# Softmax over 32,768 columns on one core: two pieces of 8192 a tile, one half scaled by VectorE and the other by ScalarE, stores at the end of the tile

## Chip, cores, metric

One core of a Trainium2 chip. The metric is device time in microseconds (us). The engines are named as the profile names them: DVE is VectorE, ACT is ScalarE, POOL is GpSimd, SP is SyncE; SPq and ACTq are their queues that issue DMA transfers.

## The reference

```python
logits: float32 [16, 256, 32768], temperature = 1.0
scaled = logits / temperature
scaled = scaled - scaled.max(axis=-1, keepdims=True)
e = np.exp(scaled)
out = e / e.sum(axis=-1, keepdims=True)
```

Every element is read once and written once: 536.87 MB in, 536.87 MB out.

## The kernel before

The 4,096 rows are cut in halves of 16,384 columns, one half to a partition, so 64 tiles of 128 x 16384 (8.39 MB). Three buffers take turns. For each piece of a tile DVE finds the negated maximum and ACT takes the exp in place with its sum. Then the two halves of a row are combined by a few one-column operations, and the pieces are scaled in place, partly by DVE and partly by ACT.

```python
_BUFS = 3
_LOAD = (8192, 8192)                    # loads of a tile, columns
_PIECES = (4096, 4096, 4096, 4096)      # pieces for max and exp
_ON_DVE = (4096, 1024, 4096, 1024)      # of each piece, scaled by DVE; ACT has the rest
_HALF = 8192                            # a store
...
    for k in range(K):                  # per piece
        nc.vector.tensor_reduce(out=nm[:, k:k+1], in_=xc, axis=X, op=A.max, negate=True)
        nc.scalar.activation(out=xc, in_=xc, func=Exp, bias=nm[:, k:k+1],
                             scale=inv_t, accum_out=ssum[:, k:k+1])
    ...                                 # small steps -> f[:, k], one factor a piece
    for k in range(K):
        a, b, c = at[k], at[k] + on_dve[k], at[k] + sizes[k]
        if b > a: nc.vector.tensor_scalar_mul(out=xs[:, a:b], in0=xs[:, a:b], scalar1=f[:, k:k+1])
        if c > b: nc.scalar.activation(out=xs[:, b:c], in_=xs[:, b:c], func=Copy, scale=f[:, k:k+1])
        if t == G - 1: store(t, a, c)
        elif t and c % _HALF == 0: store(t, c - _HALF, c)     # on ACT's queue
...
    for t in range(G):
        normalise(t)
        if t and t + _BUFS - 1 < G:
            load(t + _BUFS - 1)         # on SP's queue, into the buffer of tile t - 1
```

The first and last tile have cuts of their own, which the change leaves alone.

## Time and profile before

| | before |
|---|---|
| median, four runs | 2,493.23 us (2,493.11 to 2,493.26) |
| span in the profile | 2,491.5 us |
| DVE / ACT busy | 1580.1 us (63%) / 1352.5 us (54%) |
| DMA | 431 GB/s, both queues together 100.0% of the 16 engines' time |
| one tile in mid-run | 38.7 us |

The page, the chain of waits and the groups by form stand in the prediction. One more view: the timeline of one tile's scaling (start, length, engine, operation).

```profile
480.57 5.94 DVE L148 TENSOR_SCALAR x<-x,f 128x4096 f32<-128x4096 f32 x4
480.62 2.86 ACT L152 ACTIVATE x<-x,f 128x3072 f32<-128x3072 f32 x1 [1.15 <-DVE f L144]
483.66 0.34 ACTq L81 DMA_DIRECT2D out_dram<-x  x1
484.05 2.86 ACT L152 ACTIVATE x<-x,f 128x3072 f32<-128x3072 f32 x1 [0.56 <-DVE x L148]
...
486.93 0.34 ACTq L81 DMA_DIRECT2D out_dram<-x  x1
```

The four DVE scalings take 5.94 us together. The first store is issued when both engines have finished the first half, 3.27 us before the second store.

### The profile page before, as it was taken

The numbers are of one execution on the slowest core, as the hardware profiler recorded it, in microseconds if no ns is written. First come the engines' busy times: TensorE is split into PE (matmuls) and PEld (weight loads), VectorE is DVE, ScalarE is ACT, GpSimd is POOL, SyncE is SP. The second block draws the span as 40 slices with busy tenths as digits, with TensorE's granted clock in tenths as the row PEclk, the third lists the DMA queues.
The fourth block names the chain that finished last, engine by engine and source line by source line (L and its number), as shares of the span: only waits on it lengthen the run. The fifth ranks groups of instructions, "written<-read, shape, count | busy, mean of one in ns | idle before, by whom it ended". The sixth has DMA issues, their size and how long they took to land.

```text
span 2491.5 us, 2807 instructions
## 1 busy us (share of the span) xinstructions
DVE 1580.1 (63%) x1217; ACT 1352.5 (54%) x711; POOL 0.2 (0%) x4
## 2 busy tenths in 40 slices
DVE  7765666655766657566675666756667566665654
ACT  6565555655556555555555554555545555465544
POOL 0000000000000000000000000000000000000000
DMA  9999999999999999999999999999999999999998
GB/s 412 436 430 436 431 435 431 433 433 430 437 430 437 430 436 430 437 429 436 431 436 431 434 432 432 434 431 436 430 437 429 437 430 436 430 437 430 436 431 370
DMA packets 38038, 1073.94 MB, mean 431 GB/s; under 512 B 4224, under 2 KB 4224, under 8 KB 4224
## 3 DMA queue, kind: packets, MB, share of 16 engines
q1 hardware_dynamic: 20160, 553.66, 51.6%
q10 hardware_dynamic: 17856, 520.10, 48.4%
q14 instruction: 22, 0.18, 0.0%
HBM read 536.87 MB, written 536.87 MB: 431 GB/s over the span
## 4 chain that ended last, share of the span: by engine, by line
DMA 68%; another core or an unknown queue 15%; DVE 11%; ACT 4%; issue 1%; SPq 0%; ACTq 0%
DMA out_dram<-x 41%; DMA x<-in_logits_dram 28%; DVE nm L108 8%; ACT x L115 3%; DVE x L148 3%; SPq L72 0%; DVE f L144 0%; ACT x L152 0%; ACT ee L129 0%; DVE rS L143 0%; DVE Sh L91 0%; DVE Sh L88 0%; DVE ttj L132 0%; ACTq L197 0%
## 5 line engine op out<-in xcount | busy, mean ns | idle before, releaser
L108 DVE TENSOR_REDUCE nm<-x 128x1 f32<-128x4096 f32 (+1 forms) x257 | 1119.1, 4395 | 639.0 <-DMA x<-in_logits_dram 639.0
L115 ACT ACTIVATE x<-x,nm 128x4096 f32<-128x4096 f32 (+1 forms) x257 | 949.3, 3694 | 976.4 <-DVE nm L108 976.0
L152 ACT ACTIVATE x<-x,f 128x3072 f32<-128x3072 f32 (+1 forms) x132 | 366.4, 2781 | 129.9 <-DVE f L144 73.5
L148 DVE TENSOR_SCALAR x<-x,f 128x1024 f32<-128x1024 f32 (+3 forms) x256 | 379.9, 1548 | 2.3
L132 DVE CUSTOM_DVE_ANT_0 ttj<-ee,ssum 128x4 f32<-128x4 f32 x64 | 10.4, 162 | 228.2 <-ACT ee L129 228.2
L115 ACT ACTIVATION_READ_ACCUMULATOR x<-x,nm 128x1 f32 x257 | 47.9, 186 | 0.0
L129 ACT ACTIVATE ee<-nm,nMh 128x4 f32<-128x4 f32 x64 | 18.0, 282 | 0.0
L144 DVE TENSOR_SCALAR f<-ee,rS 128x4 f32<-128x4 f32 x64 | 14.7, 229 | 2.2
L143 DVE RECIPROCAL rS<-Sh 128x1 f32<-128x1 f32 x64 | 10.5, 164 | 2.2
L91 DVE TENSOR_TENSOR Sh<-Sh 128x1 f32<-128x1 f32 x64 | 10.2, 159 | 2.2
L91 DVE TENSOR_TENSOR nMh<-nMh 128x1 f32<-128x1 f32 x64 | 10.2, 159 | 2.2
L127 DVE TENSOR_REDUCE nMh<-nm 128x1 f32<-128x4 f32 x64 | 10.0, 157 | 2.2
L88 DVE STREAM_SHUFFLE Sh<-Sh 128x1 f32<-128x1 f32 x64 | 9.7, 151 | 0.0
L88 DVE STREAM_SHUFFLE nMh<-nMh 128x1 f32<-128x1 f32 x64 | 9.7, 151 | 0.0
L115 ACT ACT_TABLE_LOAD x1 | 1.3, 1283 | 8.1 <-DMA x<-in_logits_dram 8.1
L132 DVE DVE_READ_ACCUMULATOR2_ANT Sh<- 128x1 f32 x64 | 5.2, 82 | 0.0
L88 DVE LOAD_MASK_SELECT nMh<-nMh x64 | 0.9, 14 | 2.8
L88 DVE LOAD_MASK_SELECT Sh<-Sh x64 | 0.9, 14 | 2.8
L183 POOL MEMSET const-bfloat16-1.0<- 128x1 bf16 x1 | 0.1, 101 | 0.0
L183 POOL MEMSET const-uint8-127<- 128x1 uint8 x1 | 0.1, 101 | 0.0
L183 POOL MEMSET const-float32-0.0<- 128x1 f32 x1 | 0.1, 98 | 0.2 <-issue 0.2
L183 POOL MEMSET const-float32-1.0<- 128x1 f32 x1 | 0.1, 98 | 0.0
## 6 DMA issues: line engine op xcount, KB each, us to landing
x<-in_logits_dram SPq DMA_DIRECT2D x124, 4096.0 KB, 31.3
out_dram<-x ACTq DMA_DIRECT2D x124, 4096.0 KB, 49.3
x<-in_logits_dram SPq DMA_DIRECT2D x7, 2048.0 KB, 20.6
out_dram<-x SPq DMA_DIRECT2D x2, 4096.0 KB, 33.5
out_dram<-x SPq DMA_DIRECT2D x3, 2048.0 KB, 17.3
x<-in_logits_dram SPq DMA_DIRECT2D x2, 1024.0 KB, 36.1
out_dram<-x SPq DMA_DIRECT2D x2, 1024.0 KB, 22.8
```

The costliest lines, as they stand in the source:

```text
L88: nc.vector.stream_shuffle(out=v[:, j + 1 : j + 2], in_=v[:, j : j + 1], mask=mask)
L91: nc.vector.tensor_tensor(out=v[:, j + 1 : j + 2], in0=v[:, j : j + 1], in1=v[:, j + 1 : j + 2], op=op,)
L108: nc.vector.tensor_reduce(out=nm[:, k : k + 1], in_=xc, axis=X, op=A.max, negate=True)
L115: nc.scalar.activation(out=xc, in_=xc, func=Exp, bias=nm[:, k : k + 1], scale=inv_t, accum_out=ssum[:, k : k + 1],)
L127: nc.vector.tensor_reduce(out=nMh[:, 0:1], in_=nm, axis=X, op=A.min)
L129: nc.scalar.activation(out=ee, in_=nm, func=Exp, bias=nMh[:, n_rounds : n_rounds + 1], scale=-1.0)
L132: nc.vector.tensor_tensor_reduce(out=ttj, in0=ee, in1=ssum, scale=1.0, scalar=0.0, op0=A.mult, op1=A.add, accum_out=Sh[:, 0:1],)
L143: nc.vector.reciprocal(out=rS, in_=Sh[:, n_rounds : n_rounds + 1])
L144: nc.vector.tensor_scalar_mul(out=f, in0=ee, scalar1=rS)
L148: nc.vector.tensor_scalar_mul(out=xs[:, a:b], in0=xs[:, a:b], scalar1=f[:, k : k + 1])
L152: nc.scalar.activation(out=xs[:, b:c], in_=xs[:, b:c], func=Copy, scale=f[:, k : k + 1])
L183: nc = _bacc.Bacc("TRN2", target_bir_lowering=False, num_devices=1)
```

## The change

The intent, in the words that came with it: two column pieces of 8192 a tile, one half scaled by VectorE, the other by ScalarE; loads and stores in 32 KB halves (per partition) on two hardware queues. Fewer and longer instructions, and no half that waits for both engines.

```diff
-_PIECES = (4096, 4096, 4096, 4096)
-_ON_DVE = (4096, 1024, 4096, 1024)
+_PIECES = (8192, 8192)
+_ON_DVE = (8192, 0)
 _HALF = 8192
+_SECOND_PIECES = (4096, 4096, 4096, 4096)
+_SECOND_ON_DVE = (4096, 4096, 2048, 0)
@@ the cuts of a tile
+        if t == 1:
+            return _SECOND_PIECES, _SECOND_ON_DVE, _LOAD
         return _PIECES, _ON_DVE, _LOAD
@@ the end of normalise
-            elif t and c % _HALF == 0:
-                store(t, c - _HALF, c)
+        for h in range(0, W if 0 < t < G - 1 else 0, _HALF):
+            store(t, h, h + _HALF)
```

(The width of the small tiles, `K`, also takes in the second tile's cut.)

More of the change, by code (lines that the diff above doesn't have):

```diff
@@ L48 @@
     n_rounds = _SPLIT.bit_length() - 1
-    K = max(len(_FIRST_PIECES), len(_PIECES), len(_LAST_PIECES))
+    K = max(
+        len(p) for p in (_FIRST_PIECES, _SECOND_PIECES, _PIECES, _LAST_PIECES)
+    )
     pool = ctx.enter_context(tc.tile_pool(name="fixed", bufs=1))
```

## The prediction

> **What bounds the kernel now.** I first read the page's busy shares, its slices and its DMA queues.
>
> ```profile
> DVE 1580.1 (63%) x1217; ACT 1352.5 (54%) x711; POOL 0.2 (0%) x4
> ...
> DMA  9999999999999999999999999999999999999998
> GB/s 412 436 430 436 431 435 431 433 433 430 437 430 437 430 436 430 437 429 436 431 436 431 434 432 432 434 431 436 430 437 429 437 430 436 430 437 430 436 431 370
> ...
> q1 hardware_dynamic: 20160, 553.66, 51.6%
> q10 hardware_dynamic: 17856, 520.10, 48.4%
> ...
> HBM read 536.87 MB, written 536.87 MB: 431 GB/s over the span
> ```
>
> No compute engine is busy for two thirds of the span. The 16 DMA engines are at 90% or more in every slice but the last, and the packets of the two queues add up to 51.6 + 48.4 = 100.0% of the engines' time. Only the first and last slices (412 and 370 GB/s) are clearly below the rest. So DMA is the bound, and I ask whether a queue is ever empty. For that I read the DMA queue's own waits and, for two rounds of the three buffers, the chain that ended last.
>
> ```profile
> SPq L72 <- DMA out_dram<-x: 2339.5, 122, 47.8
> ...
> 367.60 48.28 DMA out_dram<-x
> ...
> 416.34 18.89 another core or an unknown queue
> ...
> 435.35 31.34 DMA x<-in_logits_dram
> ...
> 466.71 8.76 DVE nm L108 x2
> ...
> 475.49 3.80 ACT x L115 x2
> ...
> 480.57 3.03 DVE x L148 x2
> ...
> 483.66 48.37 DMA out_dram<-x
> ```
>
> The first row says that SyncE spends nearly the whole run waiting for a store to free a buffer. The pieces (start, length) give the loop: a first-half store issued at 367.60 lands at 415.9; the queue then issues a first-half load (0.33 us), and 18.89 us later the second-half load at 435.35, because the second-half store has landed; that load takes 31.34 us; two maxima, an exp, the small steps and scaling follow, and the next store goes at 483.66. From 367.60 to 483.66 three tiles have passed: 38.69 us a tile. A tile moves 16.777 MB (1,073.74 MB over 64), so the rate in this stretch is 16.777 / 38.69 = 433.6 GB/s.
>
> **Slack.** Loads are issued at 416.01, 435.35, 454.69 and 474.04 (the timeline of SyncE's queue): 19.35 us apart, which is what a 4.19 MB half takes when two queues share 433.6 GB/s (4.19 / 0.2168 = 19.35). A load that lands after 31.3 us has therefore queued for 12.0. A first-half store takes 48.3 us, so it has queued for 29. A second-half store is issued about 3.3 us later (448.24 against 444.97 in the timeline) and lands 19.3 us later than its first half, so it takes about 64.4 and has queued for 45. Both queues have a backlog at every moment; the stores' is the longer, by far.
>
> [...]Two hardware queues were in use already, with the same 4 MB halves.[...]
>
> **The change, part by part.** The durations come from the groups by form:
>
> ```profile
> L108 DVE TENSOR_REDUCE nm<-x 128x1 f32<-128x4096 f32 x255 | 1114.7, 4412 | 639.0 <-DMA x<-in_logits_dram 639.0
> L115 ACT ACTIVATE x<-x,nm 128x4096 f32<-128x4096 f32 x255 | 945.3, 3707 | 976.4 <-DVE nm L108 976.0 <-ACT x L152 0.5
> L152 ACT ACTIVATE x<-x,f 128x3072 f32<-128x3072 f32 x124 | 354.0, 2856 | 127.6 <-DVE f L144 71.2 <-DVE x L148 34.1 <-DMA x<-in_logits_dram 22.4
> L148 DVE TENSOR_SCALAR x<-x,f 128x4096 f32<-128x4096 f32 x124 | 291.4, 2350 | 2.2
> L148 DVE TENSOR_SCALAR x<-x,f 128x1024 f32<-128x1024 f32 x124 | 92.7, 747 | 0.0
> ```
>
> Each operation has a constant and a slope. Max: 4412 at 4096 and 2275 at 2048 (last tile) give 1.043 ns an element, so 8.69 us at 8192. Exp: 3707 and 1986 give 0.840, so 7.15 us. DVE scaling: 2350 and 747 give 0.522, so 4.49 us. ACT scaling: 2856 at 3072 and 1564 at 1536 give 0.841, so 7.16 us.
>
> (1) Engine work for each of the 61 tiles from the third to the one before the last. DVE before: 4 x 4.41 + 2 x 2.35 + 2 x 0.75 = 23.85; after: 2 x 8.69 + 4.49 = 21.87; 1.98 less, 121 us in the run, so DVE should fall to about 1,459 us. ACT before: 4 x (3.71 + 0.19 for reading the accumulator) + 2 x 2.86 = 21.29; after: 2 x (7.15 + 0.19) + 7.16 = 21.84; 0.55 more, 34 us, so about 1,386. Five instructions go on each engine in each of these tiles, and one more on DVE in the second tile: DVE 1217 to 911, ACT 711 to 406. None of this is on the path that sets the end.
>
> (2) From the second half's landing to the stores. Before: 483.66 - 466.71 = 17.0 us to the first store, 20.2 to the second. After: max 8.69, exp 7.15, the same 1.4 of small steps (exp end 479.2 to scaling 480.6), then ACT's 7.16: 24.4 us. The first half needs only DVE's 4.49, but both store issues now stand behind ACT's scaling in ACT's program order. So the first store goes 7.5 us later, the second about 4.6 (24.7 against 20.2). This is the only real cost, and it comes out of 29 and 45 us of queueing: about 21 and 40 are left. The landing times, and with them loads and period, do not move. Gain and loss in steady state: 0.
>
> (3) The start: tile 0 and its stores are untouched. Tile 1's stores move from 63.7 and 67.0 to about 66.4, behind tile 0's stores, of which the first lands at 85.0. No gap.
>
> (4) The end: the last tile is untouched. Tile 61's stores wait in ACT's queue for a late load (22.4 us in the row of ACT scaling), and in the changed program the same semaphore wait stands there. In this stretch ACT's copy moves ahead of that wait, which balances the longer exp: tile 62's stores go about 1 us earlier by the same durations. The end is then set by the last load's landing at 2,446.98 us and by the drain. About 0.
>
> (5) A small gain that I assume without proof. Three-tile steps in the chain are of two kinds: 367.60 to 483.66 is 116.06, but 250.45 to 367.60 is 117.15. Eight of the steps are long, 233 or 350 us (two or three steps) apart. The page has 22 instruction transfers on queue 14, and DVE's 1,217 instructions would need one every 262 us if each brought 128[...]. If they cause the extra 0.9 us, 911 instructions have some two or three fewer: 2 us.
>
> Sum: 2,493.3 + 0 + 0 + 0 - 2 = 2,491 us.
>
> **Rivals.** *The later stores starve the DMA engines.* For it: 7.5 us later in each tile would be up to 61 x 7.5 = 458 us if the path were serial, 2,950 us; the chain does run through max, exp and scaling. Against it: the chain's store and load pieces contain 29 and 12 us of queueing, so those steps are not a bound although the chain lists them. *The coarser pieces relieve the engines and give time back.* 121 us off DVE would be 2,372 us[...].[...] *A new bound in an engine*: in series a tile takes DVE 17.4 (maxima) + 7.15 + 1.4 + 4.5 = 30.5 us before the next tile's maximum can start, against the 38.7 of DMA: 8 us remain, so no. *A start or end that drains worse*: the last slice has few transfers left, and a wait that shifts there by some us is paid in full; 5 us either way.
>
> **Range and chances.** [...]the three runs of before differ by 0.06 us, so only the two ends and the long steps can move the time. I take 2,491 with 2,486 to 2,497. A change of 2% is 50 us; [...]a loss needs a starved queue (1%). Within 2%: 98.7%.
>
> **What would show it.** Right: DMA rate and slices as before, 38.7 us a tile; loads still 31.3 us from issue to landing; first-half stores near 41 us instead of 48.3 and second-half ones near 60; DVE near 1,459 and ACT near 1,386 us busy; the wait of SyncE for stores still over 2,300 us. The long steps should come some 350 us apart if instruction transfers cause them. Wrong: slices with DMA under 9 or 420 GB/s in mid-run, a load landing within 20 us of its issue (a queue run dry), or a period above 39 us.

What the page of the kernel before shows is that packets take 100.0% of the DMA engines' time and that no slice exceeds 437 GB/s. The 128 instructions a transfer of step (5) were assumed there; the trace of the changed kernel shows 126 to 130 (below).

## The result, and the profile after

| | before | after |
|---|---|---|
| median, four runs each | 2,493.23 us | 2,491.32 us (2,491.30 to 2,491.41) |
| ratio | | 0.9993, 95% interval 0.9975 to 1.001 |
| span in the profile | 2,491.5 us | 2,489.5 us |
| instructions DVE / ACT | 1217 / 711 | 911 / 406 |

A ratio is the mean time of one kernel's fast runs over the mean of the other's fast runs of the same rounds, so it is not quite the ratio of the medians. The kernel is the same within noise; the 1.9 us between the two is far above the scatter of these four runs (0.15 us), and below what the interval resolves.

The page of the changed kernel, busy shares, slices and queues:

```profile
DVE 1483.5 (60%) x911; ACT 1391.5 (56%) x406; POOL 0.2 (0%) x4
...
DMA  9999999999999999999999999999999999999998
GB/s 412 437 430 434 434 431 436 431 436 431 434 432 431 436 430 435 432 434 432 431 436 431 436 430 436 432 431 436 431 435 430 435 432 432 435 432 435 431 433 384
...
q14 instruction: 16, 0.13, 0.0%
...
x<-in_logits_dram SPq DMA_DIRECT2D x124, 4096.0 KB, 31.4
out_dram<-x ACTq DMA_DIRECT2D x124, 4096.0 KB, 44.6
```

DMA looks as before: 90% or more in every slice but the last. The line of q14 counts transfers of the kind that the profile names instruction: 16, where the kernel before had 22. The last two lines give the median time from issue to landing: 31.4 us for loads as before (31.3), and 44.6 for stores in place of 49.3. The two kernels move the same data.

The chain that ended last, two rounds of the three buffers (start, length, what), to be laid beside the piece in the prediction:

```profile
371.39 44.59 DMA out_dram<-x
...
416.36 18.93 another core or an unknown queue
...
435.35 31.38 DMA x<-in_logits_dram
...
466.75 8.70 DVE nm L114
...
475.47 7.21 ACT x L121 x2
...
483.96 4.50 DVE x L154
...
488.48 43.67 DMA out_dram<-x
```

The second-half load is issued at 435.35 in both kernels and lands within 0.04 us of the same moment, 466.75 against 466.71. Between that landing and the first store lie 21.7 us in place of 17.0, and the store then takes 43.7 us in place of 48.4: what the engines took longer, the store queued less. From 371.39 to 488.48 is 117.1 us for three tiles, a long step; the next ends at 604.53, 116.05 later, so 38.7 us a tile as before.

The timeline of the scaling of that tile:

```profile
483.96 4.49 DVE L154 TENSOR_SCALAR x<-x,f 128x8192 f32<-128x8192 f32 x1
484.02 7.12 ACT L158 ACTIVATE x<-x,f 128x8192 f32<-128x8192 f32 x1 [1.15 <-DVE f L150]
...
488.48 3.03 ACTq L87 DMA_DIRECT2D out_dram<-x  x2
```

The first store is issued at 488.48, the moment DVE's scaling ends, while ACT is still busy with its own until 491.14. The store instruction stands behind that ACTIVATE in ACT's program, and yet it is issued 2.66 us before the ACTIVATE ends. The second store follows at 491.17, when ACT's scaling is done (the row merges the two).

The end of the run, in stretches of 2 us (the last two columns are the DMA share and GB/s); first before, then after:

```profile
2484.00:2486.00 2.00, 0.00 (x0) 0.00 (x0) 0.00 (x0) 1.00 0.18 78
2486.00:2488.00 2.00, 0.00 (x0) 0.00 (x0) 0.00 (x0) 1.00 0.17 70
2488.00:2490.00 2.00, 0.00 (x0) 0.00 (x0) 0.00 (x0) 1.00 0.08 33
```

```profile
2482.00:2484.00 2.00, 0.00 (x0) 0.00 (x0) 0.00 (x0) 1.00 0.31 131
2484.00:2486.00 2.00, 0.00 (x0) 0.00 (x0) 0.00 (x0) 1.00 0.18 78
2486.00:2488.00 2.00, 0.00 (x0) 0.00 (x0) 0.00 (x0) 1.00 0.08 33
```

All 16 DMA engines together move 433 GB/s, so one of them moves 27 on average. In the three stretches shown of each run the DMA share is 0.18, 0.17 and 0.08 before, and 0.31, 0.18 and 0.08 after: 16 times the share is 3 to 5 engines' work, then little more than one's. In the changed kernel this tail lies 2 us earlier. The last load lands 2.0 us earlier too (2,445.02 against 2,446.98), and from there both kernels need 44.5 us.

**Where the 1.9 us come from.** The 19 three-tile steps of the chain (from the store issued at 134.26 us before, at 139.14 after) hold eight long ones (about 117.05 us against 116.13) before and six after. They sum to 2,213.8 and 2,212.6 us, 1.1 us of the difference; another 0.9 lies between the last second-half landing in these steps (2,331.08 before, 2,330.06 after) and that of the last load. The packed trace of the changed kernel has each of the 16 transfers as one packet of 8,192 bytes. Seven of them start after 53, 180, 306, 432, 559, 689 and 815 recorded DVE instructions, 126 to 130 apart, so about 128 for each; seven others lie 124 to 131 ACT instructions apart. That they bring the instructions of DVE and of ACT is read from this spacing. The long steps of the changed kernel are 349 or 350 us apart (once 465); 128 instructions at 14 a tile of 38.7 us are 354 us. Before they were 233 or 350 us apart, for a computed 262 at 19 a tile. So the spacing of the long steps fits DVE's instruction count, which the experiments had to test.

### The profile page after: what moved, and what is told of

Same layout as the page of the kernel before. It is cut to its first block, busy times and chain, and to the rows that moved or that the text cites. A ratio compares the mean times of both kernels' runs of the same rounds, so it can differ in the third digit from the quotient of the medians.

```text
span 2489.5 us, 2075 instructions
## 1 busy us (share of the span) xinstructions
DVE 1483.5 (60%) x911; ACT 1391.5 (56%) x406; POOL 0.2 (0%) x4
## 3 DMA queue, kind: packets, MB, share of 16 engines
q10 hardware_dynamic: 17856, 520.10, 48.4%
## 4 chain that ended last, share of the span: by engine, by line
DMA 63%; another core or an unknown queue 15%; DVE 14%; ACT 7%; issue 0%; SPq 0%; ACTq 0%
DMA out_dram<-x 35%; DMA x<-in_logits_dram 27%; DVE nm L114 9%; ACT x L121 6%; DVE x L154 4%; SPq L78 0%; DVE f L150 0%; ACT x L158 0%; ACT ee L135 0%; DVE rS L149 0%; DVE Sh L97 0%; DVE Sh L94 0%; DVE ttj L138 0%; ACTq L203 0%
## 5 line engine op out<-in xcount | busy, mean ns | idle before, releaser
L121 ACT ACTIVATE x<-x,nm 128x8192 f32<-128x8192 f32 (+1 forms) x135 | 913.5, 6767 | 992.0 <-DVE nm L114 976.7
L114 DVE TENSOR_REDUCE nm<-x 128x1 f32<-128x8192 f32 (+1 forms) x135 | 1112.0, 8240 | 531.6 <-DMA x<-in_logits_dram 531.6
L158 ACT ACTIVATE x<-x,f 128x8192 f32<-128x8192 f32 (+2 forms) x71 | 452.5, 6382 | 73.4 <-DVE f L150 73.4
L154 DVE TENSOR_SCALAR x<-x,f 128x8192 f32<-128x8192 f32 (+3 forms) x72 | 291.1, 4052 | 2.3
L138 DVE CUSTOM_DVE_ANT_0 ttj<-ee,ssum 128x2 f32<-128x2 f32 (+1 forms) x64 | 10.3, 161 | 430.3 <-ACT ee L135 430.3
L121 ACT ACTIVATION_READ_ACCUMULATOR x<-x,nm 128x1 f32 x135 | 25.2, 187 | 0.0
L135 ACT ACTIVATE ee<-nm,nMh 128x2 f32<-128x2 f32 (+1 forms) x64 | 17.9, 280 | 0.0
L150 DVE TENSOR_SCALAR f<-ee,rS 128x2 f32<-128x2 f32 (+1 forms) x64 | 14.6, 229 | 2.2
L97 DVE TENSOR_TENSOR Sh<-Sh 128x1 f32<-128x1 f32 x64 | 10.2, 160 | 2.2
L97 DVE TENSOR_TENSOR nMh<-nMh 128x1 f32<-128x1 f32 x64 | 10.2, 159 | 2.2
L133 DVE TENSOR_REDUCE nMh<-nm 128x1 f32<-128x2 f32 (+1 forms) x64 | 9.9, 155 | 2.2
## 6 DMA issues: line engine op xcount, KB each, us to landing
x<-in_logits_dram SPq DMA_DIRECT2D x124, 4096.0 KB, 31.4
out_dram<-x ACTq DMA_DIRECT2D x124, 4096.0 KB, 44.6
```

Of the source, the lines that this page charges most:

```text
L97: nc.vector.tensor_tensor(out=v[:, j + 1 : j + 2], in0=v[:, j : j + 1], in1=v[:, j + 1 : j + 2], op=op,)
L114: nc.vector.tensor_reduce(out=nm[:, k : k + 1], in_=xc, axis=X, op=A.max, negate=True)
L121: nc.scalar.activation(out=xc, in_=xc, func=Exp, bias=nm[:, k : k + 1], scale=inv_t, accum_out=ssum[:, k : k + 1],)
L133: nc.vector.tensor_reduce(out=nMh[:, 0:1], in_=nm, axis=X, op=A.min)
L135: nc.scalar.activation(out=ee, in_=nm, func=Exp, bias=nMh[:, n_rounds : n_rounds + 1], scale=-1.0)
L138: nc.vector.tensor_tensor_reduce(out=ttj, in0=ee, in1=ssum, scale=1.0, scalar=0.0, op0=A.mult, op1=A.add, accum_out=Sh[:, 0:1],)
```

## The experiments

Two theories were open. **Backlog**: both DMA queues always hold queued work, so nothing on the engines reaches the end (against it: the serial chain, in which each step counts). **Instructions**: the remaining 2 us come from fewer transfers of DVE instructions. All kernels gave correct results. "Before" is the kernel before in the same rounds, on the same chip.

| run | median, us | before, us | ratio | 95% interval |
|---|---|---|---|---|
| e1_widths | 2,492.10 | 2,493.24 | 0.9997 | 0.9982 to 1.0011 |
| e2_split | 2,492.94 | 2,493.24 | 0.9998 | 0.9983 to 1.0013 |
| e3_late_stores | 2,496.27 | 2,493.24 | 1.0010 | 0.9994 to 1.0027 |
| e4_two_buffers | 2,615.23 | 2,493.24 | 1.0490 | 1.0469 to 1.0511 |
| e5_dve_plus6us | 2,492.27 | 2,493.49 | 0.9995 | 0.9979 to 1.0012 |
| e6_dve_plus12us | 2,677.65 | 2,493.49 | 1.0739 | 1.0723 to 1.0755 |
| e7_instr_dve | 2,510.84 | 2,493.49 | 1.0072 | 1.0057 to 1.0087 |
| e8_instr_act | 2,503.42 | 2,493.49 | 1.0037 | 1.0022 to 1.0052 |
| e9_instr_pool | 2,495.00 | 2,494.14 | 1.0004 | 0.9986 to 1.0022 |
| e10_small_on_pool | 2,490.55 | 2,494.14 | 0.9986 | 0.9974 to 0.9999 |
| e11_instr_dve_half | 2,502.65 | 2,494.14 | 1.0034 | 1.0021 to 1.0048 |

One run each of e9 and e11 was slow (2,556.8 and 2,556.2 us); it is in the median and not in the ratio. Without it the medians are 2,494.15 and 2,502.6.

### The two parts alone

The widths alone, on the kernel before:

```diff
-_PIECES = (4096, 4096, 4096, 4096)
-_ON_DVE = (4096, 1024, 4096, 1024)
+_PIECES = (8192, 8192)
+_ON_DVE = (5120, 5120)
```

> Only the pieces of 8192 (scaling still shared inside each half, 5120 on DVE and 3072 on ACT, each half stored as soon as it is scaled). Backlog theory (DMA always has queued work, so nothing on the engines reaches the end): 2,491 to 2,493 us, 38.7 us a tile, loads 31.3 us to landing. Rival, serial chain (the 3.4 us longer exp per tile is paid): 61 x 3.4 = 207 us more, 2,700. Instruction theory (0.85 us for each 128 DVE instructions): 15 DVE instructions a tile against 14 in the changed kernel and 19 in the one before, so 2,491.8.

The 0.85 us is an estimate from the recorded 2 us: 306 DVE instructions fewer are 2.4 transfers of 128.

And the scaling split with the stores at the end, pieces of 4096 as before:

```diff
-_ON_DVE = (4096, 1024, 4096, 1024)
+_ON_DVE = (4096, 4096, 0, 0)
@@ the end of normalise: the stores as in the changed kernel
```

> Only the scaling split (first half on DVE, second on ACT) and both stores at the end; pieces stay 4096. Backlog theory: 2,491 to 2,493.5 us. Serial rival: both stores of a tile some 3 to 5 us later, 61 x 1.5 to 61 x 5 more, 2,580 to 2,800. Instruction theory: 17 DVE instructions a tile, 2,492.6.

Both lie within 0.4 us of the number from the instruction count (2,491.8 and 2,492.6 expected, 2,492.1 and 2,492.9 measured), and 87 us and more below every serial figure. The order of four kernels by DVE instructions (911, 969, 1093, 1217) is their order by time (2,491.3, 2,492.1, 2,492.9, 2,493.2). Such small differences are inside the intervals; the order alone proves little, so the doses below are larger.

### How much delay the engines may have

A useless maximum before the scaling, 5632 or 11264 elements wide, in each of 61 tiles of the changed kernel:

```diff
+        if 2 <= t <= G - 2:
+            nc.vector.tensor_reduce(out=junk, in_=xs[:, 0:5632], axis=X, op=A.max)   # e6: 0:11264
         for k in range(K):
             a, b, c = at[k], at[k] + on_dve[k], at[k] + sizes[k]
```

> The changed kernel with a useless max over 5632 elements (5.97 us by the measured 1.06 ns) on DVE before the scaling of each of 61 tiles. Backlog theory: DVE's own cycle grows from 30.4 to 36.4 us, below the 38.7 of DMA, so 2,491.3 to 2,493. Serial rival: 61 x 6.0 = 364 us more, about 2,855.

> The same with 11264 elements (11.9 us). Backlog theory: DVE's cycle of 30.4 becomes 42.3 us, 3.6 above DMA's 38.7, so DVE is the bound: 61 x 3.6 = 220 us more, 2,680 to 2,740, and DVE waits for loads hardly at all. Serial rival: 61 x 11.9, about 3,220.

Six us a tile, 361 us of added DVE time (1844.3 against 1483.5 us busy), cost nothing that can be measured: 2,492.3 us, against 2,491.3 for the changed kernel on another chip. Twelve cost 186 us over the changed kernel. The chain of e6 shows why:

```profile
992.84 17.20 DVE nm L115 x2
...
1010.06 7.21 ACT x L122 x2
...
1018.51 11.80 DVE junk L153
...
1030.34 4.49 DVE x L157
1034.82 8.59 DVE nm L115
```

No DMA is left in it: two maxima, the exp, the added maximum and the scaling follow each other, 41.98 us from 992.84 to 1034.82, and DVE waited only 12.2 us for loads in the whole run (531.6 in the changed kernel). I had expected a cycle of 42.3 and 220 us; with 41.98 the excess is 3.28 us a tile, 200 us for 61; why the run paid 14 us less is not shown. The measured 2,677.7 lies just under the range that I had given (2,680 to 2,740). The bound changed hands where DVE's cycle of 30.4 us plus the addition passes 38.7, between the two doses. So the slack in DVE has the size that the prediction worked out, about 8 us.

### How much delay the stores may have, and what the third buffer does

```diff
 # e3: the stores of a tile after both exps of the next one
+            if 2 <= t <= G - 2 and k == K - 1:
+                for h in range(0, W, _HALF):
+                    store(t - 1, h, h + _HALF)
...
-        for h in range(0, W if 0 < t < G - 1 else 0, _HALF):
+        for h in range(0, W if t == G - 2 else 0, _HALF):

 # e4
-_BUFS = 3
+_BUFS = 2
```

> The changed kernel, but both stores of a tile are issued only when the next tile's second exp has begun, some 26.7 us later for the first half and 24 us for the second. A first-half store of the changed kernel queued 43.7 - 19.35 = 24.3 us, so the store queue now runs dry for a moment in each tile. If DMA needs only one of its two queues filled: 2,491 to 2,497 us, first-half stores 17 to 25 us to landing. If a dry store queue costs time: 2.4 us a tile, about 2,640. Serial rival: 61 x 26.7 more, about 4,100.

> The changed kernel with two buffers of a tile in place of three. Backlog theory: a buffer's loop of two tiles has 77.4 us and needs at least 19.3 us of load, 24.4 of max, exp and scaling and 19.3 of store at the full rate, 63 in all, so it fits: 2,491 to 2,560 us, with shorter times to landing. Rival: the latencies of the trace (31.4 us for loads, 22 of engines, 43.7 to 60 for stores, 116 in all) are real costs that three buffers hide, so two buffers give 116 / 2 = 58 us a tile, about 3,700.

In e3 a store comes some 25 us later in each tile, and the run is 5 us longer, not 150 or 1,600. Its transfers, from issue to landing (median, in us, last):

```profile
x<-in_logits_dram SPq DMA_DIRECT2D x124, 4096.0 KB, 24.2
out_dram<-x ACTq DMA_DIRECT2D x124, 4096.0 KB, 30.5
```

In the changed kernel they are 31.4 and 44.6. The delay came out of the queueing of the stores and partly of the loads, which I had not expected: the stores stayed above the 17 to 25 us that I had given, and the loads queued less. So the work may wait in either queue.

In e4 my estimate was too kind: 2,615 us, above the 2,560 at which I had put the upper end, though nowhere near the 3,700 of the rival. Its queues and transfers:

```profile
q1 hardware_dynamic: 20160, 553.66, 52.4%
q10 hardware_dynamic: 17856, 520.10, 46.1%
...
x<-in_logits_dram SPq DMA_DIRECT2D x124, 4096.0 KB, 19.8
out_dram<-x ACTq DMA_DIRECT2D x124, 4096.0 KB, 25.4
```

A load lands 19.8 us after its issue, near the 19.35 us that a half takes at half the rate: by this estimate there is no queue of loads left. The packets' time is 52.4 + 46.1 = 98.5% of a span of 2,616.9 us, 2,578 us; in the changed kernel it is 100.0% of 2,489.5. So the same bytes took 88 us more packet time, and the DMA engines stood idle for 39 us (1.5%). My sum of 63 us in a loop of 77 had counted neither: with no backlog, the packets themselves took longer. e6 shows the same (48.5 + 46.8 = 95.3% of 2,675.8, so 2,550 us of packets). Why a packet takes longer then is not shown.

### What instruction transfers cost

```diff
+        if 2 <= t <= G - 2:
+            for i in range(28):                                    # e11: 14
+                nc.vector.memset(junk[:, i : i + 1], 0.0)          # e7, e11
+                nc.scalar.activation(out=junk[:, i : i + 1],       # e8 instead
+                                     in_=nMh[:, 0:1], func=Copy)
+                nc.gpsimd.memset(junk[:, i : i + 1], 0.0)          # e9 instead
```

> The changed kernel with 28 useless one-column memsets on DVE in each of 61 tiles (1,708 instructions, 13.3 transfers of 128 instructions). Instruction theory ([...]0.85 us for each transfer): 11 us more, 2,502, with long three-tile steps far more often. Rival (instruction transfers cost nothing and the 2 us came from elsewhere): 2,491 to 2,492.

> The same 28 useless instructions a tile, on ACT. [...]only what goes beyond DVE's is paid: 2,491 to 2,497. If any instruction transfer holds up the whole stream: 2,502. If none does: 2,491 to 2,492.

> The changed kernel with 28 useless one-column memsets a tile on GpSimd (1,708 instructions, 13 transfers more). [...]If every instruction transfer holds up the stream alike: as with DVE's, 2,503 to 2,511. ACT's 28 gave 2,499.6 to 2,504.6, so something between is possible.

> Half the dose of useless DVE instructions, 14 a tile (854 more, 6.7 transfers). Instruction theory at 0.93 us each: 6.2 us more, 2,497.5. If the 28 cost 19.5 us by something else that sets in late (a wait that the memsets bring about): less than half, 2,492 to 2,495, or, in proportion, 2,501.

The numbers: in e8 2,491 to 2,497 if ACT's transfers are paid only beyond DVE's; in e9 2,491 to 2,494 for the case that GpSimd's transfers stay behind DVE's and are not paid. The 0.93 us of e11 and e10 is an estimate like the 0.85, near the 0.92 by which the long steps before exceed the short ones (117.05 and 116.13).

The 28 memsets add 22 us to DVE's busy time (1505.8 us), where e5 added 361 for nothing. Yet e7 is 19.5 us longer than the changed kernel, and e11, with half the dose, 11.3 (by the medians, on different chips; by the two ratios to before it is 19.7 and 10.2). So it is the number of instructions and not their work, and it is about in proportion. Per 128 instructions, about one transfer, this is 19.7 / 13.3 = 1.5 us, and the same for 10.2 / 6.7, more than the 0.85 to 0.93 that I had expected. The chain of e7 and its last stretches show both parts of it:

```profile
724.34 43.51 DMA out_dram<-x
841.39 43.55 DMA out_dram<-x
958.50 43.50 DMA out_dram<-x
```

```profile
2474.00:2478.00 4.00, 0.79 (x8) 3.24 (x5) 0.00 (x0) 1.00 0.70 303
2478.00:2482.00 4.00, 3.93 (x5) 3.61 (x3) 0.00 (x0) 1.00 0.35 147
2502.00:2504.00 2.00, 0.00 (x0) 0.00 (x0) 0.00 (x0) 1.00 0.06 25
2504.00:2506.00 2.00, 0.00 (x0) 0.00 (x0) 0.00 (x0) 1.00 0.07 29
2506.00:2508.00 2.00, 0.00 (x0) 0.00 (x0) 0.00 (x0) 1.00 0.07 29
```

The first eleven three-tile steps are now all long (117.03 to 117.11 us; the later ones scatter from 116.1 to 120.0), as they should be with 42 DVE instructions a tile, 126 in three tiles: 0.95 us for each transfer in mid-run. The rest is at the end: a DMA share of 0.06 to 0.07, about one sixteenth, and 25 to 29 GB/s for 6 us and more, and before it a hole (147 GB/s) in which the last tile waits. And the rate dips in mid-run, to 427 GB/s in the 24th of the page's slices of 62.75 us, which begins at 1,443 us:

```profile
GB/s 415 431 433 434 434 433 434 433 431 433 434 434 434 434 432 430 434 434 434 433 434 431 430 427 428 429 432 434 432 427 434 432 434 434 427 434 430 431 374 339
```

The reading that fits this, an estimate from these numbers: at each transfer of DVE's instructions the landings of the loads slip by about 0.95 us, while the stream goes on as long as loads are queued. The queue of loads is 12.0 us (31.3 - 19.35), so the rate should dip when the slips have used it up. In e7 the dip comes after some 12 transfers (1,443 us at one in 117), when the landings are 12 x 0.95 = 11.4 us behind; in e11 it comes in the 34th slice (428 GB/s, from 2,063 us), after 2,063 / 177 = 11.7 transfers, 11.1 us; in e3, whose loads queue for only 24.2 - 19.35 = 4.9 us, in the 35th to 38th (423 to 429, from 2,122 us), after 2,122 / 354 = 6.0 transfers, 5.7 us. Single slices are weak evidence, since the kernel before has one of 429 GB/s too; over longer stretches e7 moves 433 GB/s from 1,000 to 1,440 us and 430 from there to 1,880, and e11 433 from 1,600 to 2,060 and 427 from there to 2,440.

The packed trace can test the reading. It keeps 16 landing records for each 4 MB transfer. The load issued at 435.35 has its eighth record at 464.7 and its sixteenth at 466.7, and DVE's maximum, which waits for this load, starts at 466.75, after the last of them. Call the time from the eighth to the sixteenth record the lag. In the loads of the changed kernel it is a staircase: 0.3 us up to 97 us, then seven steps of 0.9 to 1.0 us, 6.6 us at 2,233 us, and nearly level in between. Each of the seven steps falls on a load in whose flight an instruction transfer began (at 97.9, 449.7, 799.0, 1,148.4, 1,519.6, 1,877.7 and 2,227.1 us); the others before 2,400 us move the lag by 0.4 us at most. The packet of such a transfer is recorded at 0.31 us only, a third of the step.

In the last load the eighth record comes at 2,443.5 us in both kernels, the sixteenth at 2,451.9 before and at 2,449.9 after: the bulk of the stream is not faster, and the 2 us lie in its late end alone. In e7 the last load's eighth record comes 14.8 us later than in the changed kernel and its lag is 11.4 in place of 6.4 us, together the 19.8 us by which this load lands later; in e11 they are 6.5 and 4.8 us. Which DMA engine wrote which record, and which carried the instructions, is not shown.

Whether the lags from the transfers of several engines' instructions add up, or the largest counts, is what e8 (ACT) and e9 (GpSimd) tell. In e8 the chain's steps are regular:

```profile
955.41 44.20 DMA out_dram<-x
1072.17 44.21 DMA out_dram<-x
1188.97 44.21 DMA out_dram<-x
```

They are 116.8 us, 0.65 more than the short steps of about 116.15, with about 123 ACT instructions in each (3 x (13 + 28)), about one transfer's; and the run is 12.1 us longer at the end: ACT's instructions cost as well, less than DVE's 19.5 and more than the 6 I had allowed. By the time alone (2,503.4) the rival of the expectation, that any instruction transfer holds up the whole stream (2,502), fits better; e9 decides between them. In e9, with 1,708 memsets on GpSimd that wait for nothing in the program, the first 100 us have 13 instruction transfers; in the changed kernel they have one. The chain of e9, and below it that of the changed kernel:

```profile
145.15 46.01 DMA out_dram<-x
...
1771.59 46.01 DMA out_dram<-x
1887.76 46.01 DMA out_dram<-x
```

```profile
139.14 44.49 DMA out_dram<-x
```

The third tile's store is 6.0 us late in e9, although the bytes moved by 100 us are almost the same (41.79 and 41.95 MB): the landings are late and the stream is not. From there each of 15 steps is 116.17 us, with no long one, though DVE's program is that of the changed kernel; at the end the profiled run is 2.0 us longer, not 6.0. Lags that do not add, of which the largest counts, give just this. The landing records show it directly: from 104 to 1,866 us the lag of e9's loads stays at 6.4 us, and only then, when DVE's staircase has grown past it, does it rise, to 6.8 and 7.7 us. The fast timed runs of e9 (2,493.7 to 2,495.9, for the 2,491 to 2,494 that I had expected if GpSimd's transfers are not paid) are noisier than the effect.

### An attempt at a faster version

If DVE's instructions set the last 7 us, fewer of them should help. The products and sums of the small steps and the last factor went to GpSimd, in the changed kernel's middle tiles (edit abridged):

```diff
-        nc.vector.tensor_tensor_reduce(out=ttj, in0=ee, in1=ssum, ..., accum_out=Sh[:, 0:1])
-        combine(Sh, A.add)                                     # shuffle and add, both on DVE
+        nc.gpsimd.tensor_tensor(out=ttj, in0=ee, in1=ssum, op=A.mult)
+        nc.gpsimd.tensor_tensor(out=Sh[:, 0:1], in0=ttj[:, 0:1], in1=ttj[:, 1:2], op=A.add)
+        combine(Sh, A.add, nc.gpsimd.tensor_tensor)            # shuffle on DVE, add on GpSimd
         nc.vector.reciprocal(out=rS, in_=Sh[:, n_rounds : n_rounds + 1])
-        nc.vector.tensor_scalar_mul(out=f, in0=ee, scalar1=rS)
+        nc.gpsimd.tensor_scalar_mul(out=f, in0=ee, scalar1=rS)
```

> An attempt at a faster version: the product, its sum, the pair sum and the final factor of each middle tile on GpSimd, so 10 DVE instructions a tile in place of 14 (911 - 244 = 667), and 244 more on GpSimd. Instruction theory: 1.9 transfers fewer at 0.93 us, so 2,489.5 us; the longer small steps on GpSimd (a few us a tile) are covered by the backlog. Rival: GpSimd's latency or its own transfers give it back: 2,491 to 2,493.

2,490.55 us (2,490.1 to 2,490.9), with 667 DVE instructions. Its ratio to before is 0.9986, that of the changed kernel 0.9993 on another chip; 0.0007 is 1.7 us, the size expected, but not a difference these intervals resolve. In absolute time it is 0.8 us below the changed kernel.

## Why the prediction was right

**The bound, and the sum.** 2,491.0 was predicted and 2,491.32 measured. The claim that the backlog hides the engines is shown by doses on both sides: 6 us more DVE time a tile free, 12 us paid at DVE's own cycle, both parts alone free, stores 25 us later nearly free. SyncE still waited 2,348 us for stores, as foretold (over 2,300).

**(1) Engine work.** The instruction counts were exact (911, 406), and so were the durations (maximum 8683 ns, exp 7121, scalings 4486 and 7123, for 8.69, 7.15, 4.49 and 7.16 us). ACT came to 1391.5 for 1,386. DVE came to 1483.5 for 1,459, because I subtracted rows of single durations from a busy time that counts overlap once: two maxima in a row take 8.74 and not 8.82 us, four scalings 5.94 and not 6.19. That is 2 x 0.08 + 0.25 = 0.4 us a tile, 25 us.

**(2) The stores' delay.** This step was wrong in one term. I let the first store wait for ACT's scaling, 7.5 us later than before; it was 4.8 (21.7 against 17.0 us), because ACT's queue issued it at 488.48, while the ACTIVATE ran until 491.14. I had assumed that it would wait for the end. The second store moved by 4.2 us for 4.6. So first-half stores take 43.7 us and not 41; second-half ones take 60.3, as foretold (near 60). Nothing hung on it, since 24 us of queueing were left.

**(3), (4) Start and end** moved by nothing that shows: 44.5 us from the last load's landing in both kernels. Tile 62's first store went 2.3 us earlier, 1 us of it because landings were by then 1 us earlier.

**(5) The small gain** was assumed without proof, and its size was right: 1.9 us for 2. That it came so near is partly luck, since the lag grows by whole steps: e5, with only 61 DVE instructions more, ended one step further behind (7.5 against 6.4 us at the last load) and 0.95 us later. The long steps came 350 us apart as foretold, and e7, e8, e9 and e11 show that added instructions do cost time (19.5, 12.1, 2.0 and 11.3 us; the 2.0 of e9 by its profiled run). The prediction named no mechanism for it, and the runs show only part of one: the last landing record of a load comes later by 0.9 to 1.0 us at each of seven transfers, 6.4 us behind the eighth in the last load, and the 2 us between the kernels lie in this lag (8.4 against 6.4).

**What stays open.** Why a transfer costs 0.95 us for DVE and 0.65 for ACT; what in the DMA engines delays the last record; and whether e10's gain over the changed kernel is real.

## What to carry to other kernels

Before crediting a change with saved engine time, take the bare transfer time out of the DMA latencies in the chain; what remains is queueing, by the author's estimate, and here delays near or below it were almost free (in e3 the stores go some 25 us later, against 24.3 of queueing, for 5 us in the whole run). A chain that runs through engines does not make them the bound: add a dose of work and see (6 us a tile on DVE were free, 12 cost 186 us). In this stream the 2 us between the kernels were in the parts of a load that landed last, and 1,708 short instructions, 22 us of DVE's busy time, cost 19.5 us although DVE was busy for only 60% of the span.
